# Compression MLP in four stretches, the delta rule's row factors by shuffle, and compressed weights × values as one stacked bfloat16 matmul

## The chip, the cores and the metric

The kernel runs on one core of a Trainium2 chip. The metric is the device time of one execution in microseconds (us): the median of several runs. The five engines of the core are named as the profile names them: PE (TensorE's matmuls), PEld (its weight loads, which overlap PE), DVE (VectorE), ACT (ScalarE), POOL (GpSimd), and SP, which here only issues DMAs. "Issue" of a DMA is an instruction of an engine's queue (SPq, POOLq); the transfer itself runs beside it.

## What is computed

The reference is one layer of a decoder block on x of 256 tokens × 1024. Cut to what the change touches:

```
h = x @ w_in                                   # 1024 -> 8744, split into all the inputs below
# gated delta rule, 8 heads, 4 chunks of 64 tokens
decay  = exp(where(incl, g_i - g_j, -inf))
lower  = where(strict, (k_beta @ k.T) * decay, 0);  a_mat = lower + I
sol    = triangular_solve(a_mat, [v_beta, k_beta*exp(g)])        # u, w
state, o: scan over the 4 chunks with q @ k.T * decay, u, w
# sparse attention, 8 heads on 2 key/value groups
kc = partial_rope(silu(blk_k @ w1k) @ w2k);  vc = silu(blk_v @ w1v) @ w2v    # 15 compressed blocks
q, k_sel, k_win = partial_rope(...)            # first 32 of 128 features of each head
o = gate0 * softmax(q kc) vc + gate1 * softmax(q k_sel) v_sel + gate2 * softmax(q k_win) v_win
y = sig(g_dn)*(y_dn @ W_dn) + sig(g_nsa)*(o @ W_nsa);  x = LN(alpha*x + y @ W_out)
x = LN(alpha*x + ConvGLU(x))
```

All inputs and the output are float32.

## The kernel before

All weights come in chunks of 128×1024 float32 (512 KB). A plain chunk is loaded by SP into a ring of six tiles `raw` (`dma_chunk`, L167), split into a rounded part `hi` (ACT, L187) and a rest `lo` (DVE, L192) in rings of three, and multiplied in three passes, hi·X, hi·X_lo and lo·X, eight times over (L313 to L315: 24 matmuls with 256 columns each). `ahead()` splits the next chunk as soon as the PE has finished one; `feed()` issues the loads.

The order of the chunks is written out in `head_plan()` (L51) and `plan()`: keys and queries of the delta rule, the inputs `kc`, `vc` of the compression MLP, then a body of 16 chunks (`nq` 0 to 7, `ksl` 0 and 1, `kwn` 0 and 1, `vt` 0 to 3), after each of which one `cmp` chunk stands, then `v`, `z`, the merge gates, the branch and output projections and the ConvGLU. A `cmp` chunk is a slice of the compression MLP's first layer. It is not split: `cmp_chunk` (L767) multiplies it in float32, four matmuls with 32 columns of weights each, which go to four strips of 32 rows of one PSUM tile `ph` (L775, two instructions for each matmul). Its loads go to four slots in the tile `AT` (L171), up to four ahead.

Everything else runs as Python generators beside this order. After each plain chunk (not after a `cmp` chunk) `pump()` takes every generator one step on; `wait(name)` yields as often as the tables `W` and `WAITS` say, so that a step's place in the program is counted in chunks. Each engine executes its instructions in program order, so an instruction that waits holds all behind it on its engine. Generators that matter here:

- `delta()` (L458): the row factors `rc` are transposed (L492), copied to `rrow` (L494), written to DRAM (`rscr`, L498) and read back to all partitions by two DMAs with 512 KB each (L502), into `L` and `QKT`. DVE adds a mask and a column to `L`, POOL to `QKT` (L509, L511), ACT takes the exponential (L513, L515). Then for each of 4 chunks: similarities and transposed keys (`psim` L521, `pk` L525), products on DVE (L527, L528). Then blocks of 16 are inverted on POOL (L570, L572), written to and read from DRAM (`tscr`, L577, L580), spread into `T` and `TT` by DVE, POOL and ACT (L588, L590) and put together by `level()` (L598).
- `rope()` (L719) starts after the body: SP gathers the first 32 rows of the query and key tiles with eight DMAs (L729, L731), loads the angles (L727), DVE rotates (L734 to L739), SP writes back with eight DMAs (L741, L743). Its flag releases `attention()`.
- `cmp_end(w, hp)` (L784): second layer of the compression MLP, for keys (w = 0) with `phs` at L792, for values (w = 1) into `VCC`, 15×2×128 float32 (L817, L818).
- `attention()` (L821): `soft(n)` makes scores and exponentials of one half of the tokens (qt) and one group (g); `weigh(n)` transposes the weights (L898, L907, and for the compressed ones L913) and multiplies them with the values: L917 `VCC` × `PTC` (15 rows, 512 columns, float32), L921 the other values.

PSUM tiles of one bank come from a ring of four (`ps`); the results `pg` of plain chunks have a ring of two (`ps_g`).

Of the kernel before, what the change touches and what calls it, by code (L numbers as in the profile page):

```python
# [6 lines left out]
F32 = mybir.dt.float32  # L7
F32R = mybir.dt.float32r
BF = mybir.dt.bfloat16
# [10 lines left out]
NCMP = 15  # L20
# [9 lines left out]
CP = {}  # L30
# [3 lines left out]
def _slots(table, *items):  # L34
    o = 0
    for name, n in items:
# [6 lines left out]
              ("mL", 64), ("mQ", 64), ("l16", 64), ("l32", 64), ("bm", 4), ("caus", 128), ("cmask", 30), ("sel", 30), ("ccos", 15), ("csin", 15))  # L43
N_PP = _slots(PP, ("cw", 96), ("alog", 4), ("dtb", 4), ("nw", 1), ("pe", 64), ("fcw", 132),
              ("fcb", 44), ("g1", 8), ("b1", 8), ("w2", 512))
N_PA = 169
TAIL = 7
# [3 lines left out]
def head_plan():  # L51
# [3 lines left out]
    for i, b in enumerate(body):  # L55
        seq += [b, ("cmp", i)]
# [6 lines left out]
def plan():  # L63
# [4 lines left out]
    for j in range(NFF):  # L68
        seq += [("ug", j), ("uv", j)]
        if 0 < j <= NFF - TAIL:  # L70
# [10 lines left out]
         wc=0, sv=0, wv=0, lc=0, s3=1, s4=1, ss=0, z=0, on=0, oc=1, sim=1, vb=1, rest=0, zz=1)  # L81
WAITS = dict(back0=4, ca0=2, ca1=0, cb0=2, cb1=5, expL0=0, expQ0=0, la0=2, la2=1, la3=3, later0=0, later1=1,
             later3=2, lb0=1, lb1=2, lb2=2, lb3=0, lc0=0, lc1=0, lev0=3, mask0=5, oc0=2, oc1=1, oc2=0, oc3=0,
             on0=0, p400=2, pgm0=3, rb0=4, rest0=2, rows0=1, s10=0, s30=1, s32=1, s34=0, s36=8, s37=0, s41=2,
# [12 lines left out]
class Body:  # L97
# [72 lines left out]
    def cmp_slot(self, n):  # L170
        return self.AT[:, 1024 * (n % 4):1024 * (n % 4) + 1024]  # L171
# [59 lines left out]
    def feed(self):  # L231
        held = lambda: [*self.raw, *(i for i, h in self.plain.items() if h)]
        while self.n_dma < len(GEMM) and self.n_dma - min(held(), default=self.n_dma) < 6:
            self.dma_chunk(self.n_dma)
            self.n_dma += 1
        if self.n_split >= CMP_LEAD and self.n_cmp < 16:
            while self.n_cmp < min(16, self.cmp_done + 4):
                self.nc.sync.dma_start(self.cmp_slot(self.n_cmp), self.A["w"][CMP[self.n_cmp]])
                self.n_cmp += 1

    def setup(self):
# [24 lines left out]
        self.VCC = f.tile([NCMP, 2, 128], F32, name="VCC")  # L266
# [191 lines left out]
    def delta(self):  # L458
# [4 lines left out]
        G, GL = self.G[:, 0:16], self.G[:, 16:32]  # L463
        ssb = self.VN.rearrange("p w a v -> p (w a v)")[:, 0:256]
# [30 lines left out]
        scr = self.dram.tile([2, 2, 16, 64], F32, name="rscr")  # L495
        lq = self.LT.rearrange("p (w n) -> p w n", w=4)[:, 0:4:3]
        for w in range(2):
            nc.gpsimd.dma_start(scr[w].rearrange("e u t -> u e t"),  # L498
                                rrow[16 * w:16 * w + 16].rearrange("u (e t) -> u e t", e=2))
# [965 lines left out]
```

## Time and profile before

| what | us |
|---|---|
| median of 3 runs | 576.69 (576.42 to 577.76) |
| the profiled execution | 577.12 |
| its span, first to last instruction | 575.3 |
| busy in the span: PE / DVE / ACT / POOL | 561.3 / 391.6 / 301.5 / 106.5 |

The page of the profile gives busy times and the granted TensorE clock in 40 slices. The view of waits sums who waited for whom. The timeline lists instructions in order of time, equal neighbours merged; where two PE rows follow each other, the distance of their starts is what the first one cost, since the ends of matmuls are modelled and overlap. The table of windows gives busy times by stretch.

### The profile page before, as it was taken

To read this page: it belongs to the slowest core of one execution; us is meant where nothing else is said; L and a number is where in the kernel's file an instruction comes from. 1 tells how busy PE (TensorE), PEld (TensorE's weight loads), DVE (VectorE), ACT (ScalarE), POOL (GpSimd) and SP (SyncE) were. 2 spreads that over 40 slices of the span, in tenths; PEclk is the share of its full clock that TensorE was granted. 3 is DMA by queue.
4 is the path that set the end of the run, shared out by engine and by line. 5 is a ranking of instruction groups with operands and counts; after the bars stand their busy time and mean duration, and the time that the engine had idled before them with its cause. 6 is when DMAs were issued, how large, how long until landed. Compare 5 with 4: busy or idle time off the path is not lost.

```text
span 575.3 us, 11562 instructions
## 1 busy us (share of the span) xinstructions
PE 561.3 (98%) x4589; PEld 507.5 (88%) x4589; DVE 391.6 (68%) x674; ACT 301.5 (52%) x550; POOL 106.5 (19%) x133
## 2 busy tenths in 40 slices
PE   9999999999989999999999999999999999999994
PEld 6999988877989998888988799899999999999974
DVE  2888743684986653467657477778777777778884
ACT  4655643334454556554676344375555555556651
POOL 2466601405510220003000000059000000000003
PEclk9999999999999999999999999999999999999998
DMA  8965577965763233223353635825655555555601
GB/s 306 407 250 169 165 236 248 321 220 165 253 173 107 94 111 111 75 74 111 111 185 131 236 127 174 282 78 181 219 185 185 187 184 190 189 185 179 201 7 73
DMA packets 28790, 101.87 MB, mean 177 GB/s; under 512 B 3424, under 2 KB 4224, under 8 KB 28352
## 3 DMA queue, kind: packets, MB, share of 16 engines
q1 hardware_dynamic: 27696, 96.85, 50.0%
q0 software_dynamic: 896, 3.95, 2.4%
q8 instruction: 36, 0.59, 0.4%
q10 hardware_dynamic: 144, 0.33, 0.1%
q14 instruction: 18, 0.15, 0.1%
HBM read 98.87 MB, written 1.46 MB: 174 GB/s over the span
## 4 chain that ended last, share of the span: by engine, by line
PE 82%; DVE 9%; ACT 4%; DMA 3%; issue 1%; SPq 0%; DVEq 0%; ACTq 0%
PE pg L313 18%; PE pg L314 17%; PE pg L315 17%; PE pdn L1228 3%; PE pdn L1229 3%; PE pdn L1227 3%; DMA raw<-in_w 2%; DVE lo L192 2%; PE poa L921 2%; PE ph L775 1%; PE psa L861 1%; PE pwo L963 1%; PE pwo L964 1%; PE pwo L962 1%; ACT hi L187 1%
## 5 line engine op out<-in xcount | busy, mean ns | idle before, releaser
L192 DVE TENSOR_TENSOR lo<-raw,hi 128x1024 fp32r<-128x1024 f32 (+1 forms) x147 | 178.9, 1219 | 85.9 <-ACT hi L187 82.6
L187 ACT CAST hi<-raw 128x1024 fp32r<-128x1024 f32 (+1 forms) x151 | 154.6, 1029 | 41.1 <-PE pg L314 13.4
L313 PE MATMUL pg<-X,hi 128*128 128x256 f32 x496 | 144.2, 291 | 1.7 <-DVE Z L345 1.7
L314 PE MATMUL pg<-X,hi 128*128 128x256 f32 x496 | 139.5, 281 | 0.0
L315 PE MATMUL pg<-X,lo 128*128 128x256 f32 x496 | 139.5, 281 | 0.0
L313 PE MATMUL pg<-Y,hi 128*128 128x256 f32 x400 | 113.0, 283 | 0.0
L314 PE MATMUL pg<-Y,hi 128*128 128x256 f32 x400 | 112.7, 282 | 0.0
L315 PE MATMUL pg<-Y,lo 128*128 128x256 f32 x400 | 112.5, 281 | 0.0
L313 PEld LDWEIGHTS pg<-X,hi 128*128 128x128 f32 x496 | 93.3, 188 | 10.6 <-issue 7.3
L314 PEld LDWEIGHTS pg<-X,hi 128*128 128x128 f32 x496 | 93.5, 188 | 0.3 <-issue 0.2
L315 PEld LDWEIGHTS pg<-X,lo 128*128 128x128 f32 x496 | 93.4, 188 | 0.0
L314 PEld LDWEIGHTS pg<-Y,hi 128*128 128x128 f32 x400 | 75.3, 188 | 0.3 <-issue 0.2
L313 PEld LDWEIGHTS pg<-Y,hi 128*128 128x128 f32 x400 | 75.3, 188 | 0.2 <-issue 0.2
L315 PEld LDWEIGHTS pg<-Y,lo 128*128 128x128 f32 x400 | 75.3, 188 | 0.0
L1303 POOL TENSOR_TENSOR NQ<-NQ,AT 128x512 f32<-128x512 f32 x2 | 2.6, 1294 | 159.7 <-ACT NQ L143 159.7
L1228 PE MATMUL pdn<-lo,X 128*128 128x512 f32 (+1 forms) x90 | 31.6, 351 | 0.0
L1227 PE MATMUL pdn<-hi,X 128*128 128x512 f32 (+1 forms) x90 | 31.5, 350 | 0.0
L1229 PE MATMUL pdn<-hi,X 128*128 128x512 f32 (+1 forms) x90 | 31.4, 349 | 0.0
L345 DVE SCALAR_TENSOR_TENSOR uv<-pg,ppk,uv 128x255 f32<-128x255 f32 (+1 forms) x44 | 21.2, 481 | 11.0 <-ACT uv L143 9.8
L345 DVE SCALAR_TENSOR_TENSOR cv<-pg,ppk,cv 128x255 f32<-128x255 f32 (+2 forms) x48 | 23.1, 481 | 8.0 <-ACT cv L143 6.9
L882 POOL TENSOR_SCALAR AT<-AT,sums 128x128 f32<-128x128 f32 (+1 forms) x12 | 10.9, 920 | 88.1 <-DVE sums L874 51.0
L1267 ACT CAST X<-ug 128x256 fp32r<-128x256 f32 x22 | 8.9, 407 | 33.2 <-DVE ug L1263 33.2
(338 smaller groups left out, 932.2 us busy)
## 6 DMA issues: line engine op xcount, KB each, us to landing
raw<-in_w SPq DMA_DIRECT2D x156, 512.0 KB, 4.0
AT<-in_w SPq DMA_DIRECT2D x16, 512.0 KB, 6.6
AT<-in_first SPq DMA_DIRECT2D x3, 512.0 KB, 6.7
LT<-rscr POOLq DMA_DIRECT2D x2, 512.0 KB, 9.9
V<-in_xk POOLq DMA_DIRECT2D x1, 1024.0 KB, 5.5
KD<-in_lnp POOLq DMA_DIRECT2D x1, 1024.0 KB, 6.2
AT<-in_lnp SPq DMA_DIRECT2D x1, 1024.0 KB, 8.4
AT<-in_rope SPq DMA_DIRECT2D x1, 768.0 KB, 5.9
```

The lines of the kernel that those rows point to most:

```text
L187: nc.scalar.copy(hi[:, o:o + n], raw[:, o:o + n])
L192: nc.vector.tensor_tensor(lo[:, :n], raw[:, :n], hi[:, :n].bitcast(F32), op=OP.subtract)
L313: nc.tensor.matmul(pg, hi[:, k], src[:, 0, k], start=(k == 0), stop=False)
L314: nc.tensor.matmul(pg, hi[:, k], src[:, 1, k], start=False, stop=False)
L315: nc.tensor.matmul(pg, lo[:, k], src[:, 0, k], start=False, stop=(k == 7))
L345: nc.vector.scalar_tensor_tensor(dst[:, s:], pg[:, :S - s], cw[:, n - 1 - s:n - s], dst[:, s:], op0=OP.mult, op1=OP.add)
L882: (nc.vector, nc.gpsimd)[b].tensor_scalar(e, e, w, None, op0=OP.mult)
L921: nc.tensor.matmul(po, self.VT[:, b % 2, c0:c0 + 128], PT[:, b].rearrange("p i q -> p (i q)"), start=False, stop=(b == bs[-1]))
L1227: nc.tensor.matmul(p, fh[:, ts], hi[:, sl], start=(j == 0), stop=False)
L1228: nc.tensor.matmul(p, fh[:, ts], lo[:, sl], start=False, stop=False)
L1229: nc.tensor.matmul(p, fl[:, ts], hi[:, sl], start=False, stop=(j == NFF - 1))
L1267: nc.scalar.copy(fh, f)
```

## The change

Four things are changed.

1. The body is ordered in four stretches: four plain chunks, then four `cmp` chunks in a row. Their slots become six (two in the tile `Z`), and `feed()` issues one `cmp` load ahead of the plain loads in each call; it is no longer called in `cmp_chunk`.
2. The delta rule's chain. The row factors are read back to two partitions of each half only (2×8 KB for each half), and `stream_shuffle` on DVE copies them to the 32 partitions of each quarter. The mask and the column are added beforehand on POOL in a scratch tile (`KD`), so that DVE has one shuffle and one addition for each of `L` and `QKT`. Before it POOL clears 2048 columns. The step comes two pumps earlier (`mask0` 5 to 3), the exponential of `QKT` one pump after that of `L` (`expQ0` 1). The round trip of the inverse blocks is cut in halves (four DMAs for two) and its spreading goes to DVE and ACT alone, one pump later than before counted from the DMA (`back0` 5).
3. The rotation starts inside the body, after `kwn` 1, and not behind it: ACT copies the first 32 rows out of PSUM a second time when each chunk is evacuated (12 copies), which takes the place of the eight gathering DMAs; the angles are a third as large and are loaded at `nq` 0; DVE works before the `v` chunks begin (`ra0` 1), and `rb0` is 11, so that the flag comes after the same chunk as before.
4. The compressed values and weights are each split into three bfloat16 parts. Six products of parts are stacked along the contraction: 6×15 = 90 rows, so that one bfloat16 matmul with 512 columns does the work of the float32 one. The stacked weights are made on POOL in `weigh` (six instructions), transposed by the PE as before (90 columns, not 15), the stacked values once in `cmp_end`, five pumps later than before (`vcc` 5): two POOL copies, four float32 matmuls, three ACT and four DVE instructions.

The diff, cut to its core:

```
     body += [("vt", i) for i in range(4)]
-    for i, b in enumerate(body):
-        seq += [b, ("cmp", i)]
+    for i in range(0, 16, CMP_GROUP):
+        seq += body[i:i + CMP_GROUP] + [("cmp", i + j) for j in range(CMP_GROUP)]
...
-WAITS = dict(back0=4, ... expQ0=0, ... mask0=5, ... rb0=4, ...)
+WAITS = dict(back0=5, ... expQ0=1, ... mask0=3, ... rb0=11, ra0=1, ...)      # and W: vcc=5
...
     def cmp_slot(self, n):
-        return self.AT[:, 1024 * (n % 4):1024 * (n % 4) + 1024]
+        n %= CMP_SLOTS
+        home, n = (self.AT, n) if n < 4 else (self.Z.rearrange("p h t -> p (h t)"), n - 4)
+        return home[:, 1024 * n:1024 * n + 1024]
...
     def feed(self):
+        if self.n_split >= CMP_LEAD and self.n_cmp < min(16, self.cmp_done + CMP_SLOTS):
+            self.nc.sync.dma_start(self.cmp_slot(self.n_cmp), self.A["w"][CMP[self.n_cmp]])
+            self.n_cmp += 1
         while self.n_dma < len(GEMM) and self.n_dma - min(held(), default=self.n_dma) < 6:
             self.dma_chunk(self.n_dma)
             self.n_dma += 1
-        if self.n_split >= CMP_LEAD and self.n_cmp < 16:
-            while self.n_cmp < min(16, self.cmp_done + 4):
-                ...
...
     def delta(self):
+        nc.gpsimd.memset(self.LT[:, 1024:3072], 0.0)
...
+        seed = self.LT[:, 1024:3072]
+        nc.gpsimd.dma_start(scr.rearrange("e u t -> u e t"), rrow.rearrange("u (e t) -> u e t", e=2))
         yield from self.wait("rw")
         for e in range(2):
-            nc.gpsimd.dma_start(lq[64 * e:64 * e + 64], bass.AP(..., ap=[[0, 64], [2048, 2], [1, 1024]]))
-        yield from self.wait("mask")
-        for eng, dst, m, b in ((nc.vector, L, "mL", bL), (nc.gpsimd, QKT, "mQ", Rk)):
-            ... eng: dst += mask; dst += column (two halves each)
-        yield from self.wait("expL")
-        self.act(L, L, AF.Exp)
-        yield from self.wait("expQ")
-        self.act(QKT, QKT, AF.Exp)
+            nc.gpsimd.dma_start(seed[64 * e:64 * e + 33:32], bass.AP(..., ap=[[0, 2], [1, 2048]]))
+        for w, (m, b) in enumerate((("mL", bL), ("mQ", Rk))):
+            ... nc.gpsimd.tensor_tensor(kd[:, w, us], mask, column, op=OP.add)      (two halves each)
+        yield from self.wait("mask")
+        for w, dst in enumerate((L, QKT)):
+            flat = dst.rearrange("p u j -> p (u j)")
+            nc.vector.stream_shuffle(flat, seed[:, 1024 * w:1024 * w + 1024], [0] * 32)
+            nc.vector.tensor_tensor(dst, dst, kd[:, w], op=OP.add)
+            yield from self.wait("expQ" if w else "expL")
+            self.act(dst, dst, AF.Exp)
...
     def rope(self):
-        ... eight gathering DMAs and the load of the angles on SP
-        nc.vector.tensor_tensor(co, r, co, op=OP.mult)
         nc.vector.stream_shuffle(rs, r, [(i + 16) % 32 for i in range(32)])
+        nc.vector.tensor_tensor(v3(r), v3(r), angle(0), op=OP.mult)
+        nc.vector.tensor_tensor(v3(rs), v3(rs), angle(1), op=OP.mult)
...
     def cmp_end(self, w, hp):                     # w == 1
+            self.flags.add("cmp")
+            yield from self.wait("vcc")
+            ... h6: two POOL copies of hid, repeated six times
+                    nc.tensor.matmul(pv[:, 128 * g:128 * g + 128], h6[:, c, g]..., w2[:, 1, c], ...)
+            nc.scalar.copy(vh, pv)
+            nc.vector.tensor_tensor(rest, pv, vh, op=OP.subtract)
+            nc.scalar.copy(vm, rest)
+            self.act(out, vh, AF.Copy, scale=part[:, 0:1])
+            nc.vector.scalar_tensor_tensor(out, vm, part[:, 1:2], out, op0=OP.mult, op1=OP.add)
+            nc.vector.tensor_tensor(rest, rest, vm, op=OP.subtract)
+            nc.vector.scalar_tensor_tensor(out, rest, part[:, 2:3], out, op0=OP.mult, op1=OP.add)
+            self.flags.add("vcc")
...
     def weigh(n):
+            ... six POOL instructions: eh, e6[0:3], er, em, e6[3:5], e6[5]
-                        nc.tensor.transpose(pt[:, i], ec[:, i], ident)
+                        nc.tensor.transpose(pt[:, i], e6[:, i].rearrange("p b n -> p (b n)"), ident)
...
+        def evac_rot(dst, slot):
+            def evac(pg, j):
+                nc.scalar.copy(dst(j), pg)
+                q, a = slot(j)
+                nc.scalar.copy(self.r[32 * q:32 * q + 32, 256 * a:256 * a + 256], pg[0:32])
```

## Rows read from the trace of the kernel before

**Rows 1.** The page: span, busy times, and TensorE's granted clock in 40 slices.

```profile
span 575.3 us, 11562 instructions
PE 561.3 (98%) x4589; PEld 507.5 (88%) x4589; DVE 391.6 (68%) x674; ACT 301.5 (52%) x550; POOL 106.5 (19%) x133
PEclk9999999999999999999999999999999999999998
```

**Rows 2.** Waits of PE, whole program: waiter, releaser, us in total, times, longest.

```profile
PE pg L313 <- DVE Z L345: 1.7, 1, 1.7
PE phs L792 <- DVE LT L527: 1.2, 1, 1.2
```

**Rows 3.** Timeline around one `cmp` chunk: start, us, engine, line, tiles, shapes, count.

```profile
77.68 0.28 PE L314 MATMUL pg<-X,hi 128*128 128x256 f32 x1
...
77.80 0.28 PE L315 MATMUL pg<-X,lo 128*128 128x256 f32 x1
78.01 0.22 PEld L775 LDWEIGHTS ph<-AT,misc 128*32 128x32 f32 x8
78.01 0.67 PE L775 MATMUL ph<-AT,misc 128*32 128x256 f32 x8
...
78.61 0.38 PE L313 MATMUL pg<-X,hi 128*128 128x256 f32 x1
...
78.83 0.28 PE L314 MATMUL pg<-X,hi 128*128 128x256 f32 x1
```

**Rows 4.** Timeline of PE at the first similarity step of the delta rule.

```profile
104.16 1.09 PE L521 MATMUL psim<-QK 128*64 128x128 f32 x16
105.18 0.66 PE L525 MATMUL pk<-cpk,QK 128*128 128x128 f32 x4
```

**Rows 5.** Timeline of PE at the first weighing of values.

```profile
223.30 1.12 PE L917 MATMUL poa<-AT,VCC 15*128 15x512 f32 x2
224.35 1.98 PE L921 MATMUL poa<-AT,VT 128*128 128x512 f32 x4
```

**Rows 6.** Timeline of PE at scores, a bfloat16 matmul among float32 ones.

```profile
250.92 0.27 PE L862 MATMUL psa<-causb,idb 128*128 128x256 bf16 x1
251.03 1.02 PE L861 MATMUL psa<-KC,NQ 128*128 128x512 f32 x2
```

**Rows 7.** Timeline of POOL at the reading back of the row factors.

```profile
93.91 1.18 POOL L502 DMA_DIRECT2D LT<-rscr  x2 [3.30 <-DMA rscr<-rrow]
106.27 1.72 POOL L509 TENSOR_TENSOR LT<-LT,cpk 128x512 f32<-128x512 f32 x1 [11.19 <-DMA LT<-rscr]
```

**Rows 8.** DMA issues by line: engine, count, KB each, median us to landing.

```profile
AT<-in_w SPq DMA_DIRECT2D x16, 512.0 KB, 6.6
...
rscr<-rrow POOLq DMA_DIRECT2D x2, 8.0 KB, 3.4
```

**Rows 9.** Timeline of DVE at the rotation, among the `v` chunks.

```profile
157.60 1.06 DVE L735 STREAM_SHUFFLE AT<-AT 128x768 f32<-128x768 f32 x1
158.70 0.96 DVE L737 TENSOR_TENSOR AT<-AT 128x768 f32<-128x768 f32 x1
...
160.57 1.51 DVE L345 SCALAR_TENSOR_TENSOR Z<-pg,ppk,Z 128x255 f32<-128x255 f32 x3
```

**Rows 10.** Timeline of ACT in the same stretch.

```profile
162.17 0.72 ACT L143 ACTIVATE LT<-VN,cpk 128x512 f32<-128x512 f32 x1 [4.26 <-DMA VN<-tscr]
```

**Rows 11.** DVE's splits among the `v` chunks: count, busy us, mean ns, idle before.

```profile
L192 DVE TENSOR_TENSOR lo<-raw,hi 128x1024 fp32r<-128x1024 f32 x9 | 11.0, 1227 | 2.8 <-ACT hi L187 2.8
```

**Rows 12.** Windows: stretch, length, busy PE, PEld, DVE, ACT, POOL, clock, DMA share, GB/s.

```profile
117.10:138.70 21.60, 21.60 (x161) 15.90 (x157) 13.90 (x27) 6.22 (x10) 5.26 (x12) 1.00 0.66 216
138.70:169.00 30.30, 28.56 (x262) 27.75 (x259) 26.89 (x44) 14.74 (x23) 14.31 (x25) 1.00 0.68 204
169.00:202.00 33.00, 32.75 (x444) 30.20 (x443) 21.11 (x51) 17.59 (x50) 3.19 (x4) 1.00 0.35 112
```

**Rows 13.** Groups of ACT instructions, 70 to 120 us.

```profile
L998 ACT COPY NQ<-pg 128x256 f32<-128x256 f32 x8 | 3.0, 371 | 16.9 <-PE pg L315 16.9
```

More of the change, by code (lines that the diff above doesn't have):

```diff
@@ L46 @@
 N_PA = 169
+CMP_GROUP = 4
+CMP_SLOTS = 6
 TAIL = 7
@@ L494, in delta @@
         nc.vector.tensor_copy(rrow, pr[0:32, 0:128])
[L495 to L499, printed above, removed]
+        scr = self.dram.tile([2, 32, 64], F32, name="rscr")
+        seed = self.LT[:, 1024:3072]
+        nc.gpsimd.dma_start(scr.rearrange("e u t -> u e t"), rrow.rearrange("u (e t) -> u e t", e=2))
@@ L813, in cmp_end @@
         else:
-            pv = po[0:NCMP, :256].rearrange("p (g d) -> p g d", g=2)
+            self.flags.add("cmp")
+            yield from self.wait("vcc")
+            po = self.ps("pc2")
+            rows = 6 * NCMP
+            h6 = self.AT[:, 4096:4456].rearrange("p (c g b n) -> p c g b n", c=2, g=2, b=6)
+            for c in range(2):
+                nc.gpsimd.tensor_copy(h6[:, c], hv[:, c][:, :, None, :].to_broadcast([128, 2, 6, NCMP]))
+            pv = po[0:rows, :256]
             for g in range(2):
                 for c in range(2):
-                    nc.tensor.matmul(pv[:, g], hv[:, c, g], w2[:, 1, c], start=(c == 0), stop=(c == 1))
-            nc.vector.tensor_copy(self.VCC, pv)
-            self.flags.add("cmp")
+                    nc.tensor.matmul(pv[:, 128 * g:128 * g + 128], h6[:, c, g].rearrange("p b n -> p (b n)"),
+                                     w2[:, 1, c], start=(c == 0), stop=(c == 1))
+            vh, vm = (self.PTC[0:rows, 256 * i:256 * i + 256] for i in range(2))
+            out = self.VCC.rearrange("p g d -> p (g d)")
+            rest = self.scr("vr")[0:rows, :256]
+            part = self.cp("vm")[0:rows]
+            nc.scalar.copy(vh, pv)
[6 more added lines that the diff above has]
+            self.flags.add("vcc")
     def attention(self):
@@ L916, in weigh @@
             po = self.psum.tile([128, 512], F32, name="poa", tag="c", bufs=1)
+            while "vcc" not in self.flags:
+                yield
             nc.tensor.matmul(po, self.VCC[:, g], PTC, start=True, stop=False)
@@ L1025, in run @@
                 self.feat(kind, j, X, evs[kind])
+            if (kind, j) == ("nq", 0):
+                nc.sync.dma_start(V[:, 0:2].rearrange("p h t -> p (h t)"), A["rope"])
+            if (kind, j) == ("kwn", 1):
+                self.flags.add("nsa_in")
+                self.start(self.rope())
             if (kind, j) == ("k", W["smalls"]):
@@ L1428, in _layout @@
     ct, st = angles(np.arange(S))
[L1429 removed]
+    out["rope"] = np.concatenate([np.tile(ct, (4, 1)), np.tile(st, (4, 1))], 1)
     out["cpk"] = cp
```

97 lines of the change are left out of this document (51 added, 46 removed).

## The prediction

> **What bounds the kernel now.** I read the page first: PE is busy for 561.3 of 575.3 us, the other engines for 68% at most, and TensorE's granted clock stands at 9 tenths or more in all but the last slice, its upper level [rows 1]. So the time is what PE executes plus what PE waits for. The waits of PE come next: in the stretch that the change touches, only two waits of any length are named, 1.7 us for a release by DVE among the `v` chunks and 1.2 us before `phs` [rows 2]. Together they are the most that can be won by moving work of other engines, about 3 us. All else must come out of PE's own instructions, so I then read the timeline for what these cost from start to start, since ends are modelled [rows 3 to 6]. Last, for the two waits, I looked at what DVE, ACT and POOL do there [rows 7, 9 to 12].
>
> **Four `cmp` chunks in a row.** In a plain chunk matmuls start every 0.12 us. From the last one to `ph` it is 0.21, `ph` to the next plain one 0.60, and this one to its successor 0.22 [rows 3]. So entering and leaving another shape costs 0.09 + 0.10 = 0.19 us, and the chunk itself 0.60. Of these 0.60, how much is streaming? `ph` has 8 passes of 256 columns on four strips, 512 columns in sequence; `psim` has 16 passes of 128 columns on two strips, 1024 in sequence, and takes 1.02 [rows 3, 4]. The difference, 512 columns, costs 0.42, so a `ph` chunk streams for 0.42 and pays 0.18 for its first load and for running empty. In a row only the first pays that: 12 chunks × 0.18 = 2.2 us. The 16 entries of before become 9: four groups, of which two share theirs with a step of the delta rule before them, and five steps that stood beside a `cmp` chunk and now stand alone (after `nq` 0, `nq` 2, `ksl` 1, `kwn` 0, `vt` 0). 7 × 0.19 = 1.3 us. Sum **-3.5 us**. If chunks in a row don't overlap at all, only the 1.3 remain; that is the other end.
>
> [...] The trace: the eight weight loads of a `ph` chunk are through 0.22 us after its first matmul starts, while the matmuls last 0.67 [rows 3], so second loads run beside first passes. [...]
>
> **Stacked values.** The float32 matmul of L917 costs 1.05 us from start to start, for 512 columns in two instructions [rows 5]. A bfloat16 matmul of 256 columns costs 0.11 between float32 ones [rows 6], so 512 cost 0.22, plus about 0.10 for a load that isn't hidden (the exit price above). 1.05 - 0.32 = 0.73, four times: **-2.9 us**. If the load or the change of type costs more, still the difference of the streams stays: -2.5. The transposes with 90 columns of weights keep their number and their 128 moving columns: 0. The four matmuls for the values keep theirs too, and stand with other steps instead of alone: 0 to -0.2, taken as 0. What makes the stacks lies beside PE: in `weigh` 540 elements on POOL, at 1.72 us for 512 [rows 7] 1.8 us each time, of which the transpose comes a pump later, so 0 while POOL is nearly idle (3.2 of 33 us at 169 to 202 [rows 12]). The stacked values: four DVE instructions like a third of L345's 1.51 [rows 9], three on ACT like a copy with 0.37 [rows 13], together 3.1 us in the `z` stretch, where DVE is busy for 21.1 and ACT for 17.6 of 33 us [rows 12]: 0, up to +1 where DVE is late already. DVE beside a busy POOL was not fast: I put **+0.4** for both.
>
> **The delta rule's chain.** Before, the two reads of 512 KB keep POOL waiting for 11.19 us [rows 7], then DVE and POOL add masks, ACT takes exponentials, and only then can DVE free `psim`; PE waits for that at `phs` [rows 2]. Now the read moves 32 KB. No row shows such a read: its near bound is the 8 KB write with 3.4 us [rows 8], its far one the 11.19. I take 3.4, since bytes are near to it and the read's rows no longer cover 128 partitions. The read was issued at 93.91 [rows 7]; three `cmp` chunks of 0.79 less stand before it now, so it goes at 91.5 and lands at 95, by the far bound at 103. POOL adds the masks meanwhile, 4 × 1.72 = 6.9 us, done at 99. The masks came in the pump after `ksl` 0, at 104 [rows 4], and come two pumps earlier, after `nq` 6: 104 less two chunks of 2.85 and eight `cmp` chunks of 0.79, plus a group of 2.1 and 0.4 for steps that now stand alone, is 94.5, and DVE is there once the split is done, at about 97. It needs two shuffles of 1.06 × 1024/768 = 1.41 and two additions of 0.96 × 1024/768 = 1.28 [rows 9], 5.4 us. Behind them on DVE wait the splits: the next one is done at about 104 and needed at 108, since one plain chunk more than its own is split ahead and `psim` and a group lie between. By the far bound it would be done at 110, 2 us late. The similarities of `kwn` 0 now come two in one pump and take all four PSUM tiles before `phs` asks for one: `psim`, `pk` twice is 3.2 us, and DVE frees the first about 3.7 us after the chunk's end (copy 0.37 twice, cast 1.05, split 1.23, product 0.7). So of the 1.2 us some 0.4 stay: **-0.8 us**; ends 0 and -1.2, with the far bound +1.2. POOL's clearing of 2048 columns (four times L509's size, so up to 7 us) lies before the factors, where POOL has been waiting.
>
> **The rotation.** Four DVE instructions of 0.96 to 1.06 end right before the L345 that frees `pg` at 162 us [rows 9], and PE's 1.7 us wait is for that one [rows 2]. Among the `v` chunks DVE has per chunk 1.23 + 1.51 = 2.74 us [rows 9, 11] in 24 × 0.12 = 2.85: no room for 3.9 us. It is full there, 26.9 of 30.3, but between 117 and 139 only for 13.9 of 21.6 [rows 12]. Moved there, the 3.9 us fit into 7.7 idle ones. ACT is the next one late: it was held for 4.26 us by the read of the inverse blocks, until 162.17 [rows 10]. With the chain a pump earlier and `back` a pump longer this read has some 3 us more, and the evacuation it held was not what PE waited for. The eight gathers leave SP's queue; the eight write-backs now stand before loads for which the ring of six holds chunks. The second copies add 12 × 0.37 = 4.5 us on ACT, before each cast; ACT has more than half of each chunk free there. So **-1.7 us**, ends 0 and -1.9 (with the switch of PE).
>
> **Loads.** `cmp` loads take 6.6 us to land [rows 8]. The last of a stretch is issued when the first plain chunk of the stretch has been split, 6 us or more before it is needed in the last stretch, where four `vt` chunks leave the least room: 0, up to +1.
>
> **The sum.** -3.5 - 2.9 + 0.4 - 0.8 - 1.7 = -8.5 us against the profiled execution of 577.12: 568.6. That execution is 0.43 above the median, so the median comes to **568.2**, 1.5% less.
>
> **Rivals.**
> 1. *The two waits come back elsewhere.* DVE and ACT have as much to do as before, and whichever is late next keeps PE's 2.5 us. For it: `v` leaves DVE 0.1 us a chunk. Against it: 7.7 idle us before. Time: 570.7.
> [...]
> 3. *Slower: DVE is held at its shuffle.* DVE executes in order; if the seed lands late, shuffle, splits and so PE stand behind it, one for one. From the working above PE stands from about 10 us after the issue of the read; to use up 8.5 us and lose 1.7 more (578.4), the read would have to take 20 us, nearly twice the 11.19 of the large one. A POOL that needs as long for its masks does the same. Against it: 32 KB for 1 MB. Time: 579.
> 4. *The stacked matmul is no cheaper*, because PE doesn't take it at the pace of rows 6. Then the 2.9 stay: 571.1. The 0.11 speak against it.
>
> **How the numbers follow.** Forecast 0.55; rival 1 0.17; rival 2 0.10, both together 0.05; rival 4 0.03; a mishap that eats all of it and no more (within 0.3%) 0.04; rival 3 0.06. A measurement of this kernel can tell about 0.3%, 1.7 us, from no change. So faster 0.90, same 0.04, slower 0.06. The range: below, all ends at their best: -3.5 - 2.9 - 0.2 - 1.2 - 1.9 = -9.7, without the 0.4, thus 567.0, and 1 us for the many small waits of PE between 165 and 200 us that could shrink with DVE's lead: 566.0. Above, rivals 1 and 2 together with a little more: 573.5. Outside remain about 0.15.
>
> **What would show it.** Right, step by step: on PE four groups `ph` with 32 instructions, 1.9 us from start to start; L917 as one instruction per weighing, about 0.32 to its neighbour; no wait of PE for L345 near 160, one of some 0.4 before `phs`; DVE's shuffles beginning at about 97 us without waiting for a DMA; the `v` chunks beginning at about 134 us where they began at 138.7; the rotation on DVE between the `vt` chunks; from 330 us on the same rows as before, 8 to 9 us earlier. [...]

## The result and the profile after

| | before | after |
|---|---|---|
| median, us | 576.92 (576.42 to 577.76) | 571.14 (569.71 to 573.04) |
| ratio, with 95% interval | | 0.990 (0.9875 to 0.9924) |
| profiled execution / its span, us | 577.12 / 575.3 | 570.68 / 568.9 |

The kernel is 1.0% faster: 5.8 us by the medians, 6.4 us between the two profiled spans. The forecast was 568.2 us, 8.5 us less. The result lies inside the range, two thirds of the way to the forecast, and 0.4 us from the time of rival 1 (570.7). Rival 4 (571.1) lies as near, and so do chunks in a row that don't overlap (rival 2, 568.2 + 2.2 = 570.4), so the time alone can't tell them apart; the rows have to. One run of experiment 7 took 3067.72 us and one of experiment 9 1387.43 us; the times given for these two are the medians of their other three runs.

The page of the changed kernel first: the span, the busy times and TensorE's granted clock. It answers [rows 1].

```profile
span 568.9 us, 11592 instructions
PE 554.0 (97%) x4585; PEld 508.2 (89%) x4585; DVE 394.4 (69%) x681; ACT 308.2 (54%) x568; POOL 115.0 (20%) x160
PEclk9999999999999999999999999999999999999998
```

PE has 7.3 us less to do, and the span is only 6.4 us shorter: PE still sets the end, and it waits more than before. Which waits are new is in the waits of PE (waiter, releaser, us in total, times, longest), to be read against [rows 2]:

```profile
PE psa L881 <- DVE LT L623: 2.1, 1, 2.1
PE pg L319 <- ACT V L1048: 0.9, 1, 0.9
...
PE ppt L926 <- ACT KD L146: 0.7, 1, 0.7
...
PE phs L792 <- DVE LT L534: 0.5, 1, 0.5
...
PE pr L499 <- DVE rcat L486: 0.4, 1, 0.4
```

The 1.7 us wait for the rotation has gone, the one before `phs` has gone down from 1.2 to 0.5; but 2.1 us stand at a scores matmul (`psa`) and 0.9 at a plain chunk, where nothing of any length stood before. The gains on PE show in its timeline, at the first group of four `cmp` chunks, at the second one, and at the second weighing. The distance from one start to the next is the cost.

```profile
84.27 1.97 PE L776 MATMUL ph<-AT,misc 128*32 128x256 f32 x32
86.17 0.39 PE L319 MATMUL pg<-X,hi 128*128 128x256 f32 x1
...
99.36 1.10 PE L776 MATMUL ph<-Z,misc 128*32 128x256 f32 x16
...
101.25 0.39 PE L319 MATMUL pg<-X,hi 128*128 128x256 f32 x1
...
236.94 0.39 PE L947 MATMUL poa<-PTC,VCC 90*128 90x512 bf16 x1
237.17 1.88 PE L951 MATMUL poa<-AT,VT 128*128 128x512 f32 x4
```

A group of 32 instructions takes 1.90 and 1.89 us, where four single chunks took 4 × 0.60 [rows 3]. The stacked matmul takes 0.23 us, where the float32 one took 1.05 [rows 5].

Where the difference of the spans lies, cut at points that both traces have (the first matmuls of `nq` 0 and `v` 0, the ends of the steps after `v` 7, after `z` 3 and of the last weighing):

| stretch | before, us | after, us | difference |
|---|---|---|---|
| up to `nq` 0 | 70.52 | 70.18 | -0.34 |
| `nq` 0 to `v` 0 | 68.15 | 65.45 | -2.70 |
| `v` and the first level | 27.67 | 24.57 | -3.10 |
| `z` 0 to 3 with their steps | 25.82 | 28.38 | **+2.56** |
| on to the last weighing | 136.65 | 133.70 | -2.95 |
| from there to the end | 246.49 | 246.62 | +0.13 |

The loss sits in one stretch. That the values' matmuls moved from the `v` stretch into it explains 0.94 us of the 2.56 (the row of L824 below, to its successor). The wait of 2.07 us is more than the rest, 1.62; other steps there take some 0.45 less. PE's timeline around it, and DVE's:

```profile
168.05 1.15 PE L617 MATMUL pu<-A,LT 64*64 64x64 f32 x32
169.03 1.10 PE L622 MATMUL pt<-LT,A 64*64 64x64 f32 x32
170.07 1.10 PE L824 MATMUL pc<-ppk,AT 128*90 128x128 f32 x8
171.01 0.60 PE L881 MATMUL psa<-KC,NQ 128*128 128x256 f32 x2
...
173.79 0.70 PE L881 MATMUL psa<-KC,NQ 128*128 128x256 f32 x2 [2.07 <-DVE LT L623]
```

```profile
171.91 1.23 DVE L197 TENSOR_TENSOR lo<-raw,hi 128x1024 fp32r<-128x1024 f32 x1 [2.25 <-ACT hi L192]
173.05 0.68 DVE L623 TENSOR_TENSOR LT<-LT,pt 128x512 f32<-128x512 f32 x1
```

One pump asks for five PSUM tiles: `pu`, `pt`, `pc`, `psa`, `psa`. The ring has four. The fifth gets the tile of `pt`, which DVE gives back with L623; that instruction stands behind a split that itself has waited for ACT's cast. Call a step that holds a tile a tenant of the ring. My first theory for the missing 2.1 us (8.5 forecast, 6.4 between the spans) was: **the moved values are the fifth tenant of a ring of four**. The rival: **DVE and ACT are late there in any case**, and without the values the wait would be at the next matmul. For the smaller wait of 0.87 us near 105 the theory was: **the seed of the row factors lands late, and DVE's shuffle and ACT's exponential pass that on**; the rival: ACT's second copies of the evacuated chunks (L1048, which the wait names) are what is late.

### The profile page after: what moved, and what is told of

It reads as the page before. It is cut to its first block, busy times and chain, and to the rows that moved or that the text cites. A ratio compares the mean times of both kernels' runs of the same rounds, so it can differ in the third digit from the quotient of the medians.

```text
span 568.9 us, 11592 instructions
## 1 busy us (share of the span) xinstructions
PE 554.0 (97%) x4585; PEld 508.2 (89%) x4585; DVE 394.4 (69%) x681; ACT 308.2 (54%) x568; POOL 115.0 (20%) x160
## 4 chain that ended last, share of the span: by engine, by line
PE 74%; DVE 8%; ACT 7%; DMA 4%; issue 3%; POOL 3%; SPq 0%; DVEq 0%; ACTq 0%; POOLq 0%
PE pg L319 16%; PE pg L321 16%; PE pg L320 16%; PE pdn L1270 3%; PE pdn L1271 3%; PE pdn L1269 3%; DVE lo L197 2%; ACT hi L192 2%; PE poa L951 2%; POOL VN L579 1%; PE pwo L994 1%; PE pwo L993 1%; PE pwo L992 1%; POOL itmp L577 1%; DMA VN<-tscr 1%
## 5 line engine op out<-in xcount | busy, mean ns | idle before, releaser
L197 DVE TENSOR_TENSOR lo<-raw,hi 128x1024 fp32r<-128x1024 f32 (+1 forms) x147 | 181.7, 1238 | 77.6 <-ACT hi L192 76.2
L351 DVE SCALAR_TENSOR_TENSOR uv<-pg,ppk,uv 128x255 f32<-128x255 f32 (+1 forms) x44 | 21.2, 481 | 11.0 <-ACT uv L146 9.8
L351 DVE SCALAR_TENSOR_TENSOR cv<-pg,ppk,cv 128x255 f32<-128x255 f32 (+2 forms) x48 | 23.1, 481 | 8.1 <-ACT cv L146 6.9
```

What stands on the lines that cost most here:

```text
L197: nc.vector.tensor_tensor(lo[:, :n], raw[:, :n], hi[:, :n].bitcast(F32), op=OP.subtract)
L351: nc.vector.scalar_tensor_tensor(dst[:, s:], pg[:, :S - s], cw[:, n - 1 - s:n - s], dst[:, s:], op0=OP.mult, op1=OP.add)
```

## The experiments

Each kernel is compared with the kernel before; the ratio to hold against is 0.990 (0.9875 to 0.9924) of the changed kernel. The profiled runs also differ where no edit acts: `nq` 0 begins between 70.18 and 71.60 us, since PE waits for its first load for up to 2.0 us (0.5 in the changed kernel). From `nq` 0 to the end of the span it takes 504.8 us before and 498.7 in the changed kernel; where a gain is small, this time is given too.

**1. The values five pumps later.** Here the values' stacks are written over the stacked weights of the first weighing, so this one weighing is not computed from its own weights; the amount of work is the same.

```
-         wc=0, sv=0, wv=0, lc=0, vcc=5, ...
+         wc=0, sv=0, wv=0, lc=0, vcc=10, ...
```

> The changed kernel with the stacked values made five pumps later (vcc 10 for 5), nothing else. In the changed kernel PE waits 2.07 us for a psa at 173.8, and the four PSUM tiles then have five tenants in one pump (pu, pt, the values' pc, psa, psa). Theory: the fifth tenant is the cause; without it the wait goes, against 0.2 us for a cluster of its own: about 569.3 where the changed kernel has 571.1. Rival: DVE and ACT are late in this stretch for their amount of work, whatever the tiles; then a wait of 1.5 us or more stays there and the time stays at 571.

Measured: 575.88 us, ratio 0.998 (0.9963 to 0.9997): nearly all of the gain is gone. The wait at `psa` has gone, and the steps there cost 3.33 us instead of 6.39 (from the last plain matmul before them to the first one after). But see PE and POOL where the values stand now, and the table of windows (stretch, length, busy time of PE, PEld, DVE, ACT and POOL, granted clock, DMA share, GB/s):

```profile
203.98 2.01 PE L824 MATMUL pc<-ppk,AT 128*90 128x128 f32 x8 [4.24 <-POOL AT L820]
```

```profile
200.47 3.18 POOL L902 TENSOR_SCALAR AT<-AT,sums 128x128 f32<-128x128 f32 x4 [11.52 <-DVE ec L895]
203.59 0.61 POOL L820 COPY AT<-hid 128x180 f32<-128x180 f32 x2
```

```profile
204.00:206.00 2.00, 2.00 (x9) 2.00 (x10) 0.00 (x0) 0.00 (x0) 0.38 (x2) 0.50 0.55 219
206.00:208.00 2.00, 2.00 (x11) 2.00 (x11) 0.69 (x2) 1.18 (x3) 0.00 (x0) 0.50 0.00 0
208.00:210.00 2.00, 2.00 (x14) 2.00 (x14) 1.03 (x3) 0.00 (x0) 0.00 (x0) 0.66 0.03 8
```

The copies that make the stacks are POOL's. They come at 203.59, right behind products of the weights, which themselves begin at 200.47, after 11.52 us of waiting for the softmax. PE waits 4.24 us for them. Then the granted clock is 0.50 for 4 us and 0.66 for 2 more. From the clock alone I estimate the cost at some 2.7 us (half of 4 and a third of 2); that is a little high, since plain matmuls start 0.21 us apart at 0.50 (from 206.00 on) and 0.12 apart at 1.00. The ring theory holds for the old place; the new place has a worse wait of its own.

**2. The `cmp` chunks one by one again**, the rest as changed.

```
-CMP_GROUP = 4
+CMP_GROUP = 1
```

> The changed kernel with plain and cmp chunks in turn again (a group of 1), all else kept. By the prediction the row of four is worth 3.5 us of PE's instructions (2.2 for streaming on, 1.3 for entries); against it the changed kernel has waits of 0.4 us (pr) and 0.9 us (pg, released by ACT) that a slower body may not have. So 571.1 + 3.5 - 1.3 = 573.3 or up to 574.6. Rival: chunks in a row don't overlap, then only 1.3 come back and are met by the waits: 571 to 572.4.

Measured: 575.96 us, ratio 0.9973 (0.9949 to 0.9998). From `nq` 0 to `v` 0 it takes 70.22 us instead of 65.45, 4.77 more. A new wait of 2.65 us (a `ph` for the evacuation of the one before, by ACT) and the one before `phs` (0.54) make 3.19 us of waits there, against 1.82 in the changed kernel (0.41 + 0.87 + 0.54). The streams alone differ by 4.77 - 1.37 = 3.4 us, and the term of the prediction was 3.5. The time lies above what was expected (573.3 to 574.6), since this long wait is not in that sum.

```profile
PE ph L776 <- ACT hp L781: 2.7, 1, 2.7
```

**3. Values and weights in float32 again**, without stacks and without the later pump for the values; the rest as changed.

```
-        self.VCC = f.tile([6 * NCMP, 2, 128], BF, name="VCC")
+        self.VCC = f.tile([NCMP, 2, 128], F32, name="VCC")
...
-                    nc.tensor.matmul(pv[:, 128 * g:128 * g + 128], h6[:, c, g].rearrange("p b n -> p (b n)"),
-                                     w2[:, 1, c], start=(c == 0), stop=(c == 1))
...
+                    nc.tensor.matmul(pv[:, g], hv[:, c, g], w2[:, 1, c], start=(c == 0), stop=(c == 1))
+            nc.vector.tensor_copy(self.VCC, pv)
...
-                        nc.tensor.transpose(pt[:, i], e6[:, i].rearrange("p b n -> p (b n)"), ident)
+                        nc.tensor.transpose(pt[:, i], ec[:, i], ident)
```

> The changed kernel with compressed values and weights in float32 as before (one float32 matmul per weighing, values made at the old place), all else kept. In the changed kernel L947 and its entry cost 1.0 us less per weighing than L917 did: 4.0 us come back on PE. If the 2.07 us wait at psa belongs to making the stacked values, it goes with them, and 0.2 us come for a cluster alone: 571.1 + 4.0 - 2.1 + 0.2 = 573.2. Rival, the wait belongs to the stretch and not to the stack: 575.1 or more.

Measured: 571.76 us, ratio 0.9909 (0.9888 to 0.993): the same as with the stacks, within the intervals. At a weighing the float32 matmul takes 1.05 us again, as in [rows 5]. The four weighings cost 1.01, 0.93, 1.01 and 1.01 us more from plain chunk to plain chunk: 4.0 us. But no `psa` waits for the ring, and from `nq` 0 to the end of the last weighing it takes 252.59 us, against 252.10 with the stacks. So the stacks save 4.0 us on PE and earn 0.5: 2.07 are given back at the ring, the rest in the wait for `ppt` (0.7 instead of 0.3 us) and in several small ones.

**4. The old rotation**, the rest as changed.

```
+        for j in range(4):
+            nc.sync.dma_start(r[32 * j:32 * j + 32, 0:512]..., self.NQ[0:32, 2 * j:2 * j + 2])
...
-                   nq=evac_rot(...), ksl=evac_rot(...), kwn=evac_rot(...))
+                   nq=cps(...), ksl=cps(...), kwn=cps(...))
```

> The changed kernel with the rotation as before: eight gathering DMAs, the start behind the body, no second copies out of PSUM on ACT; all else kept. Theory of the prediction: 3.9 us on DVE among the v chunks bring back a wait of PE of 1.7 to 1.9 us for L345 (573.0); if the 0.9 us wait that ACT's second copy now releases goes with the copies, 572.1. Rival: the wait before needed the late read of the inverse blocks as well, which now comes earlier; then none returns and the time is 571.1 or 0.9 less.

Measured: 573.69 us, ratio 0.9945 (0.9926 to 0.9965). `v` 0 comes at 135.13, no later than in the changed kernel, but the `v` stretch takes 29.12 us instead of 24.57. DVE at the rotation, PE right after, and the windows:

```profile
156.14 0.96 DVE L747 TENSOR_TENSOR AT<-AT 128x768 f32<-128x768 f32 x1
157.02 1.51 DVE L351 SCALAR_TENSOR_TENSOR Z<-pg,ppk,Z 128x255 f32<-128x255 f32 x3
```

```profile
158.67 0.36 PE L319 MATMUL pg<-X,hi 128*128 128x256 f32 x1 [2.90 <-DVE Z L351]
```

```profile
155.00:158.70 3.70, 0.80 (x8) 0.63 (x6) 3.56 (x7) 1.46 (x4) 0.00 (x0) 1.00 0.78 239
...
160.00:162.00 2.00, 2.00 (x12) 2.00 (x11) 1.93 (x6) 0.35 (x1) 0.00 (x0) 0.50 0.26 66
162.00:164.00 2.00, 2.00 (x34) 1.78 (x35) 1.49 (x3) 0.72 (x2) 0.00 (x0) 0.70 0.49 113
```

The wait is back, as the rotation's place on DVE says, and longer than in [rows 2] (2.90 us for 1.7), since PE comes earlier and DVE doesn't. After it the clock is at 0.50 and 0.70 for 4 us, by the same estimate some 1.6 us lost (half of 2 and three tenths of 2). There is also a wait of 1.2 us for ACT's evacuation of `nq` near 105 although this kernel has no second copies: the rival for the small wait falls.

```profile
PE pg L319 <- ACT NQ L1035: 1.2, 1, 1.2
```

**5. The values two pumps earlier**, with POOL's copies ahead of the wait and the matmuls behind it.

```
-         ... vcc=5, ...
+         ... vcc=3, ...
...
-            yield from self.wait("vcc")
-            po = self.ps("pc2")
             rows = 6 * NCMP
...
+            yield from self.wait("vcc")
+            po = self.ps("pc2")
```

> The changed kernel with the stacked values made two pumps earlier (vcc 3 for 5), between the last v and the first z chunk, and its two POOL copies before that wait. There the ring of four PSUM tiles has two tenants (pa and pc). Theory, the fifth tenant: the wait of 2.07 us at psa goes and none comes in its place: 569.0 where the changed kernel has 571.1. Rival, seven more instructions on DVE and ACT are too many behind the full v stretch: a wait of 1 us or more shows up between 157 and 175, and the time is 570 or more.

Measured: 573.02 us, ratio 0.992 (0.989 to 0.9951). The wait for L623 has gone; two others stand at the same steps, and TensorE's clock falls behind them (0.59 and 0.55 from 174 to 178). PE's waits, and ACT:

```profile
PE pt L622 <- DVE ec L872: 2.0, 1, 2.0
PE psa L881 <- ACT AT L146: 1.5, 1, 1.5
```

```profile
164.80 0.41 ACT L832 CAST PTC<-vr 90x256 bf16<-90x256 f32 x1 [3.50 <-DVE vr L831]
...
166.93 1.92 ACT L146 ACTIVATE V<-Z 128x2048 f32<-128x2048 f32 x1
168.87 0.37 ACT L1100 COPY Z<-pg 128x256 f32<-128x256 f32 x1
```

ACT waits 3.50 us for a value from DVE, and the SiLU of all of `v` and an evacuation stand behind it: the evacuation comes at 168.87, in the changed kernel the same row is at 164.65. Here the rival was right: in this place ACT and DVE have no room for the values' evacuation.

**6. The masks on DVE one pump later.**

```
-WAITS = dict(... expQ0=1, ... mask0=3, ...)
+WAITS = dict(... expQ0=0, ... mask0=4, ...)
```

> The changed kernel with DVE's shuffles and additions one pump later (mask0 4 for 3, expQ0 0 for 1), so that the first similarities stay in the same pump, but ACT has evacuated nq 7 before it comes to the exponential that waits for DVE. Theory: the wait of 0.87 us of PE near 105 is ACT standing at the exponential in front of that evacuation; it goes, and the rest stays: 570.3. Rival: DVE's lateness itself holds PE, then the wait appears one chunk later or the 0.54 us before phs grow by as much, and the time stays at 571.1.

Measured: 571.94 us, ratio 0.9901 (0.9873 to 0.9928). No wait near 105 any more, but one of 0.8 us for L351 (DVE) near 161; the 2.1 us at `psa` stay. From `nq` 0 to the end it takes 498.4 us, 0.3 less than the changed kernel: no gain that the times could show.

```profile
PE pg L319 <- DVE Z L351: 0.8, 1, 0.8
```

**7. POOL's masks ahead of the read-back**, so that POOL adds them while the seed is still being written: the two DMAs go behind the additions of L514.

```
-        yield from self.wait("rw")
-        for e in range(2):
-            nc.gpsimd.dma_start(seed[64 * e:64 * e + 33:32], bass.AP(tensor=scr.tensor, offset=scr.offset + 2048 * e,
-                                                                     ap=[[0, 2], [1, 2048]]))
...
+        yield from self.wait("rw")
+        for e in range(2):
+            nc.gpsimd.dma_start(seed[64 * e:64 * e + 33:32], bass.AP(tensor=scr.tensor, offset=scr.offset + 2048 * e,
+                                                                     ap=[[0, 2], [1, 2048]]))
```

> The changed kernel with POOL's four mask additions moved between the issue of the write of the factors and of the read, where POOL waits for 5.1 us; nothing else. In the changed kernel a split on DVE takes 3.99 us (for 1.23) while POOL adds. Theory: it is POOL's work beside it that slows it; the split then takes 1.2 to 1.3, and a split or an idle stretch of DVE at 90 to 94 takes its place. The read still lands at about 100.4, so the shuffles begin no earlier than that and the time stays at 571.1 (0.3 either way). Rival: the 3.99 are a wait of the split's own (for its hi or its buffer); then they stay.

Measured: 570.53 us, ratio 0.9891 (0.9846 to 0.9937). The profiled span is 567.7 us (497.5 from `nq` 0), and the wait near 105 is 0.3. DVE in the changed kernel, and POOL beside it:

```profile
96.86 3.99 DVE L197 TENSOR_TENSOR lo<-raw,hi 128x1024 fp32r<-128x1024 f32 x1 [1.62 <-ACT hi L192]
...
100.78 1.35 DVE L519 STREAM_SHUFFLE LT<-LT 128x1024 f32<-128x1024 f32 x1
```

```profile
94.51 1.14 POOL L507 DMA_DIRECT2D LT<-rscr  x2 [5.08 <-DMA rscr<-rrow]
95.67 2.08 POOL L514 TENSOR_TENSOR KD<-cpk,bL 128x512 f32<-128x512 f32 x2
97.70 2.06 POOL L514 TENSOR_TENSOR KD<-cpk,rcat 128x512 f32<-128x512 f32 x2
```

And DVE with the masks first:

```profile
91.21 3.47 DVE L197 TENSOR_TENSOR lo<-raw,hi 128x1024 fp32r<-128x1024 f32 x1 [2.83 <-ACT hi L192]
...
96.91 1.23 DVE L197 TENSOR_TENSOR lo<-raw,hi 128x1024 fp32r<-128x1024 f32 x1 [1.09 <-ACT hi L192]
100.16 0.01 DVE L519 LOAD_MASK_SELECT LT<-LT  x1 [2.03 <-DMA LT<-rscr]
```

The split that took 3.99 us beside POOL's additions takes 1.23 without them, and an earlier split, which now stands beside them (POOL adds from 89.49 to 93.58), takes 3.47. The shuffle (L519, which begins with the loading of its mask) still starts only 0.6 us earlier, since now DVE waits for the seed itself. Two causes lay on top of each other, and removing one leaves the other.

**8. Experiments 5, 6 and 7 together.**

> The three edits of the runs beside it together. If they touch different waits, their gains add up: 571.1 - 2.1 - 0.9 = 568.1. Rival: what is taken from one wait goes to the next; then 569 to 570.

Measured: 573.52 us, ratio 0.9929 (0.9901 to 0.9957). Up to `v` 0 it is the shortest of all so far (64.34 us from `nq` 0, against 65.45), but the waits of experiment 5 are there again (2.1 and 1.5 us), with the clock at 0.50 from 174 to 178. The early place of the values costs more than both moves of the masks bring.

**9 and 10. The values where the ring and all three engines have room.** The pumps after `z` 4 and `z` 5 have three and two tenants in the changed kernel, and POOL has nothing to do between 189.6 and 201.5. The copies go to a part of `misc`, which nothing else uses there. The masks stay ahead of the read-back as in experiment 7. The diff is that of experiment 9; experiment 10 has `vcc` 9.

```
-         ... vcc=5, ...
+         ... vcc=8, ...
...
-            h6 = self.AT[:, 4096:4456].rearrange(...)
+            h6 = self.misc[:, 1600:1960].rearrange(...)
```

> The masks are added before the seed's read is issued, and the values' four matmuls come in the pump after z chunk 4, where the changed kernel has only three tenants for the four tiles of the ring (pt and two psa, 191.39 to 192.95); their copies lie in a part of `misc` that nothing else uses before 208 us, so they overwrite no weights. Theory (the 2.07 us wait is the fifth tenant of one pump, and the other two places tried, with 2.0 + 1.5 and 4.24 us, failed for what DVE, ACT and POOL had queued there): POOL has nothing to do between 189.6 and 201.5, so no wait of 2 us or more of PE between 158 and 215, the values' cluster costs its 0.9 us and no more, time 568.5 to 569.5 (571.1 less 2.07 and up to 0.5 for the masks). Rival (DVE and ACT are late in the whole z stretch, whatever the place): the evacuation of the values, some 5 us on ACT and DVE, makes a wait of 1.5 to 2.5 us at the psa after it or at the first weighing (pc or po, near 208), time 570.5 to 572.

> The same as e9_free_pump with the values one pump later, after z chunk 5 (195.76), where the changed kernel has two tenants (a level's pv and pa) and the next pump at 203.6 is the one before the weighing. Theory: as e9, no wait at the ring, 568.5 to 569.5; POOL's next product begins at 201.5, 5 us after the copies, so they are not held. Rival: the evacuation chain, with ACT and DVE behind the level's work, ends later than the weighing at 208.5 needs it, PE waits 1 to 3 us there, time 570 to 572; a wait of about 3 us would be followed by the half clock, and the time would be 573.

Measured: 569.41 us, ratio 0.9872 (0.9838 to 0.9906), and 569.03 us, ratio 0.9863 (0.9833 to 0.9893); from `nq` 0 496.5 and 496.8 us. In neither does a `psa` wait for more than 0.2 us. In experiment 9 the `pa` of the next pump waits 0.7 us for an exponential on ACT, so its place isn't quite free. In experiment 10 a wait of 1.1 us stands near 105 again, since the seed landed later (DVE waits 2.87 us for it, and shuffles at 101.28).

**11. The values after `z` 5 alone**, masks and read-back as in the changed kernel: one number and one place are all that differs from it.

> One change against the changed kernel: the values' step after z chunk 5 instead of z chunk 1, its copies in `misc`; masks and read-back are as in the changed kernel. Theory (fifth tenant): the 2.07 us wait of PE at psa goes and nothing comes for it, the 0.87 us wait near 105 stays, span about 566.8 to 567.5, time 569 to 569.5. Rival (what e10 won came from the masks): the wait at psa or another of 1.5 us or more among the z chunks stays, time 570.5 to 571.5.

Measured: 569.37 us, ratio 0.9858 (0.983 to 0.9885). PE in the old place and in the new one:

```profile
170.83 1.10 PE L622 MATMUL pt<-LT,A 64*64 64x64 f32 x32
171.86 0.70 PE L881 MATMUL psa<-KC,NQ 128*128 128x256 f32 x2
...
172.53 0.70 PE L881 MATMUL psa<-KC,NQ 128*128 128x256 f32 x2
...
195.81 1.04 PE L824 MATMUL pc<-ppk,misc 128*90 128x128 f32 x8
196.78 1.15 PE L611 MATMUL pa<-LT 64*64 64x64 f32 x32
```

Four tenants, no wait; the values cost 0.97 us in the other pump and hold up nothing. From `z` 0 to the end of the last weighing it takes 160.14 us instead of 162.08, 1.94 less, so nearly all of the 2.07 us is won back. The two intervals overlap, so it is the rows that show this and not the times. DVE is as late as before all the same; only nothing waits for it now, since L623 begins 2.3 us after the last `psa`:

```profile
174.86 0.68 DVE L623 TENSOR_TENSOR LT<-LT,pt 128x512 f32<-128x512 f32 x1
```

So the wait of 2.07 us is there because of the fifth tenant, and how far DVE is behind PE sets its length: the same five tenants cost 1.3 us in experiments 2 and 4 and 1.8 in experiment 7.

**12. Experiment 10 with the masks on DVE one pump later** (the edit of experiment 6).

> e10_next_pump with the delta rule's masks on DVE one pump later, so that DVE and ACT aren't held by a seed that lands late. Theory (the wait of PE near 105 is the landing of the seed, 99.1 to 101.3 us so far, passed on by DVE's shuffle and ACT's exponential): no wait there, 569.0 less 0.9 to 1.1, so 568.0. Rival (DVE is full behind it, so that the same work is late at another place): the 0.8 us wait for the release of pg by DVE near 159, which e6_mask_later showed, comes back, and the time stays at 568.8 to 569.5.

Measured: 568.58 us, ratio 0.985 (0.9823 to 0.9877), span 566.1 us, 495.5 from `nq` 0. Neither the wait near 105 nor one for L351 is there. The largest wait of PE behind the start is one that the changed kernel had too:

```profile
PE ppt L926 <- ACT KD L146: 0.7, 1, 0.7
```

The 0.8 us for L351 of experiment 6 was therefore not the price of its edit: experiments 1 and 11 show 0.8 and 0.6 of it without that edit, and experiment 12 none with it. What brings it in some runs is not shown. That this kernel is faster than the changed one is likely: the two intervals just touch (0.9877 and 0.9875), and from `nq` 0 the profiled run is 3.2 us shorter.

## Why the prediction was right or wrong

The direction and the range were right, the size was a third too large. Term by term:

| term | predicted, us | measured, us | where |
|---|---|---|---|
| groups of four | -3.5 | -3.4 | experiment 2, without the waits |
| stacked matmul | -2.9 | -4.0 | experiment 3 |
| wait before `phs` | -0.8 | -0.7 | waits before and after |
| rotation | -1.7 | -1.9 | 1.7 and the entry; no wait for L351 left |
| side work of the stacks on other engines | +0.4 | +2.07, +0.4, +0.4 | `psa`; `ppt`; three small steps of 0.1 to 0.2 |
| new waits of the delta rule's chain | `pg` in the ends of the -0.8, `pr` not put down | +0.9 and +0.4 | `pg` and `pr` |
| sum | -8.5 | -5.8 | |

The spans differ by 6.4. The 0.6 that the sum of the measured terms lacks are 0.34 before the change begins and small differences that I can't assign.

**Groups.** 1.90 us for 32 instructions, as worked out (0.42 × 4 + 0.18 with the entry). The step that could have failed was whether a second chunk's first load hides beside the first one's passes; at 1.90 us for four chunks, where one alone takes 0.60, it does: all 32 weight loads are through 1.52 us after the first matmul starts. Chunks that don't overlap would have given groups of 4 × 0.60 = 2.4 us. The gain has a price that the prediction did not put down: with four plain chunks in a row `pr` comes before DVE is ready (0.4 us; the wait is not there in experiment 2, nor in experiment 4, which has no second copies on ACT).

**Stacked matmul.** Undersized by 1.1 us. The term went by the shape before and after and put down 0.32 us for the new one. It is 0.23: the bfloat16 matmul on 90 rows pays no visible entry between its neighbours of 128 rows. And the step from plain chunk to plain chunk lost another 0.2 each time, which the float32 matmul on 15 rows had cost at its borders.

**The side work: the step that failed.** "The four matmuls for the values ... stand with other steps instead of alone: 0 to -0.2, taken as 0", and their evacuation "0, up to +1 where DVE is late already". I counted PE's instructions and the other engines' idle time, and not the tiles: the step was moved into a pump that already asked for four tiles of a ring of four. The price, 2.07 us, is not that of any instruction added; it is the distance to the end of L623 in a queue on DVE. It is as large as the whole miss between the profiled spans (8.5 - 6.4), and half of what the stacks had won. That it is the whole is partly luck, since what else was mis-sized nearly cancels: the 1.1 us more that the stacked matmul won against waits of 1.7 us at `pg`, `pr` and `ppt`, of which 0.4 was put down. Rival 1 had its size (2.5 us, 570.7) but another cause: it had whichever of DVE and ACT is late next. Experiment 11 shows that without a fifth tenant the same lateness of DVE costs PE nothing; experiment 5 shows that in another place the rival's cause is real.

**The delta rule's chain.** The shuffles were to begin at 97 us and began at 100.78. Two steps failed. The write and the two reads of the seed took 5.3 us and 4.6 and 5.3 us to land, where I took 3.4, the near bound, and left the write as it was. The read was issued at 94.51 and not at 91.5: POOL waited for the write for 5.08 us and not 3.30, and the write itself went out at 88.65, only 0.7 us earlier than before. And "DVE is there once the split is done, at about 97" had the split at its usual time; beside POOL's masks it took 3.99 us. A third size was wrong and did no harm, by luck: the 1.72 us that I took for one of POOL's additions [rows 7] is that of an instruction beside additions of DVE's; the new ones take 1.05 each, and though they begin 3.5 us later than I put down, they are done at 99.8 where I had 99. What the lateness does was named rightly (splits behind the shuffle on DVE), but the first victim was not a split: it was ACT, whose exponential at 103.49 stands ahead of an evacuation of `pg`, for which PE waited 0.87 us:

```profile
103.49 1.06 ACT L146 ACTIVATE LT<-LT 128x1024 f32<-128x1024 f32 x1 [6.66 <-DVE LT L520]
```

Of the ends I gave for this term, the near one was taken because of its bytes; these 16 KB took longer to land than the median half megabyte into `raw` (3.4).

**Rotation.** Right in place and size: it runs on DVE from 130.51 to 134.4, among `vt`, and experiment 4 shows that with the rest of the change the old place would have cost 2.9 us and not 1.7. (24 × 0.12 is 2.88 and not 2.85, and 12 × 0.37 is 4.4 and not 4.5; nothing hangs on either.)

**The signs.** Lead from 330 us on: 8 to 9 us forecast, 6.5 found, and it stays to the end (the last row of the stretches: +0.13), so nothing is given back late. `v` 0 was to begin at about 134 and began at 135.63. With three steps placed elsewhere (experiment 12) the sum of the prediction is nearly reached (568.58 against 568.2), though by terms of other sizes: the stacks won more than was forecast, the waits that are left take it back.

## What to carry to other kernels

When a step is moved in a hand-made order, count besides the time of its instructions the buffers it asks for in the place that it comes to: with a ring of four the fifth tenant waits for a release that stands at the end of another engine's queue, and that can eat much of the gain (here 2.07 of the stacks' 4.0 us). Then look at what each of its instructions stands behind on its own engine in the new place (the values' copies on POOL, behind 3.18 us of products, made PE wait 4.24 us); of five places tried for one small step, one was held by POOL, one by ACT and DVE, one by the ring, one cost 0.7 us and one nothing. A saving on the engine that sets the time was kept here only where the neighbouring engines had a lead, or where nothing that PE needs hung on them. A share over the whole span doesn't show this: DVE is busy for 69% of it and ACT for 54%, and both were late around the last `v` and the first `z` chunks.

## What the runs showed of the hardware

**In four runs a long wait of PE was paid twice.** After waits of 1.7 us [rows 2], 2.07 us and 2.65 us (experiment 2) the granted clock stayed at 1.00 in the profiled runs. With 2.90 us (experiment 4), 4.24 (experiment 1) and the pair 2.0 and 1.5 (experiment 5; 2.1 and 1.5 in experiment 8) it fell, in experiments 1 and 8 while PE still waited: windows of 2 us show 0.50 in experiments 1, 4 and 8 and 0.55 in experiment 5. From the means of the windows I estimate the time at 0.50 at some 3.5 us (experiments 4 and 5) to 7 (experiments 1 and 8), at a cost, estimated from the clock alone, of about 1.6 us (experiment 4) to 2.7 (experiment 1). A rival with waits as long as these should be priced with that on top; mine were not. The windows of experiment 2, the wait and what follows it:

```profile
107.00:109.50 2.50, 0.00 (x0) 0.00 (x0) 2.30 (x3) 2.48 (x5) 0.00 (x0) 1.00 0.06 20
109.50:113.00 3.50, 3.42 (x31) 3.04 (x32) 2.49 (x4) 1.50 (x4) 0.00 (x0) 1.00 0.69 221
```

**A split on DVE took 3.99 us beside POOL's additions.** The split L197, which reads two tiles, took 3.99 us while POOL added two tiles as well, and 1.23 where POOL is idle (from 94.01 us). It ended one split's time after POOL's last mask (97.70 + 2.06 + 1.23 = 100.99; the split ended at 100.85). So it lasted from the second of four additions in a row until past the last. Experiment 7 shows the same: 3.47 us from 91.21, POOL's last mask done at 93.58, the split at 94.68. It isn't always so: from 378.71 us two splits in a row take 3.35 us in the same trace while POOL adds, and POOL's additions beside them take 1.72 and 1.61 us, where others of the same two lines take 0.74 and 0.73. What makes the difference is not shown.

**16 KB by POOL's queue took about as long to land as 512 KB by SP's.** The write took 5.3 us, the two reads 4.6 and 5.3. In the same run the medians for half a megabyte on SP's queue are 3.4 (`raw`), 6.3 (`AT`) and 8.0 (`Z`).
